# First layer of a two-layer encoder: x transposed on the host, the RMS root applied at eviction or by a spread row, the norm's weight folded into the weight tiles

## The chip, the cores and the metric

The kernel runs on 1 core of one Trainium2 chip. The metric is the device time of one execution in microseconds (us), as the median of several executions. Before the change it is 2655.88 us, the median of 3 executions from 2654.63 to 2658.3 us. One further execution was taken by the hardware profiler; its span, from the first to the last instruction, is 2652.0 us.

## The reference

The model has two layers on x of 2048 rows (frames) by 1024 columns, all in float32. Only the front of the first layer matters for the change:

```python
h = rms_norm(x, a_norm_g)                       # x * rsqrt(mean(x*x, row) + 1e-6) * g
u, v, z = jnp.split(h @ w_in, 3, axis=-1)       # w_in is 1024 x 6144; u, v, z are 2048 wide
u = jax.nn.gelu(u)
v = layer_norm(jax.nn.gelu(v), ln_g, ln_b)
mixed = w_m @ v  (per group of 128 rows, per head of 128 columns)  + b_s
x = x + (u * mixed * jax.nn.silu(z)) @ w_out
```

After that come a shared K/V projection, a chunked band attention layer and a last RMS norm, which the change leaves as they are but for one pair of small tiles.

The RMS norm multiplies each row of x by a scalar, its root, and each column by an element of the weight g. The row scalar can therefore be applied to the rows of a product instead of to the rows of its left operand, and the column weight to the rows of w_in.

## The kernel before, in words

**Products.** Every fp32 product is made of three matmuls on two-part operands: a high part rounded to TensorE's fp32r form and a low part that is the remainder (`mm3`, L110 to L114, whose three matmuls are L111, L112 and L113). `split` (L433) makes the parts: ScalarE (ACT) copies the source into the high part (L434), VectorE (DVE) subtracts it from the source into the low part (L437).

**Stage order.** The first layer's input product is done by a Strassen-Winograd scheme on 2x2 blocks: the rows are paired as even and odd blocks of 128 (16 blocks, so 8 pairs `j`), the 1024 input columns as two halves of 512, and w_in is cut in six slices `n` of 1024 columns: n = 0, 1 are v, n = 2 to 5 hold u and z. For each n there are seven products, the phases `ph`, in the order 1, 2, 6, 5, 7, 4, 3, and for each phase eight steps `j`. A step is 12 matmuls of 128x512: 4 blocks of 128 input columns times 3. For phases 1 and 2 a step of n = 0 makes the product of n = 1 too (24 matmuls). Then the slice "o" makes the layer's output product with steps of 24 matmuls. `run_steps` (L659) writes the order out: at step s it runs the events of s, then the matmuls and the eviction of s, then prepares the left operand of step s + 3 (LOOK = 3), then the weight work due at s. A scheduler at compile time turns this into one instruction queue for each engine; SyncE (SP) issues all DMAs from one queue.

**Left operands S.** With a11, a12 the halves of an even row block and a21, a22 those of the odd one, phase 1 takes a11, phase 2 takes a12, phase 4 takes a22, and phases 6, 5, 7, 3 take sums of blocks. The matmul wants them with the input columns on the partitions, so they are transposed. In n = 0 each of the 7 x 8 = 56 operands is made by `s_split` (L607): four TensorE transposes of 128x128 into PSUM (L611), a split out of PSUM into an S tile (6 buffers), and one step later a store of both parts to HBM (`hsd`, L614, 512 KB). All other steps, and the phases 7, 4 and 5 of n = 0 too, load the stored tile back (`s_load`, L600, DMA at L602).

**The norm.** `block_norm` (L692) does for each of the 16 row blocks: load 128x1024 (L697), ACT squares and sums along the row (L703), DVE adds eps (L709), GpSimd (POOL) raises to -0.5 (L710), DVE multiplies the block by the root and the weight in one instruction (L714). The weight is held as a 128x1024 tile `gab`, loaded once as a broadcast (L699). Only then can the transposes of that block run. Odd blocks go on to `block_c` and `block_d` (L728, L738): POOL makes the three sums of the Winograd scheme (L734 to L736), and the operands of phases 4 and 5 are transposed, split and stored early, during phases 1 and 2.

**Weights T.** `make_t` (L448) loads quarters of w_in (tiles `rw`, 128x1024, 512 KB, L470), combines them on POOL (`comb`, L445) where the phase wants a sum, and splits the result (L434, L437). The result lies in one of 8 buffers, that is two phases of four.

**Eviction.** `evict` (L568) takes a product out of PSUM (4 banks): ACT copies it in phase 1 (L574), DVE adds it to an accumulator in the others (L570). The accumulators are tiles `acc` of 128x512, 25 buffers. PSUM's other 4 banks hold the transposes in n = 0 and n = 1.

## Time and profile before

| | us |
|---|---|
| time of 3 executions | 2654.63, 2655.88, 2658.3 |
| span of the profiled execution | 2652.0 |
| TensorE (PE) busy in it | 2608.0 |
| DVE, ACT, POOL busy in it | 1885.1, 1303.2, 897.2 |
| first product's first matmul starts | 10.82 |

The profile lists each instruction with its engine, its line, and the tiles that it writes and reads ("out<-in"). PE's matmuls are pipelined: their shown durations overlap, so what one costs on PE's line is read from the distance between the starts of neighbours. "Idle before" is the time an engine sat idle before an instruction, with the instruction or DMA whose end released it. Windows give the busy time of each engine in a stretch, with the granted TensorE clock (1 is full speed) and the busy share of the 16 DMA engines.

### The profile page before, as it was taken

To read this page: it belongs to the slowest core of one execution; us is meant where nothing else is said; L and a number is where in the kernel's file an instruction comes from. 1 tells how busy PE (TensorE), PEld (TensorE's weight loads), DVE (VectorE), ACT (ScalarE), POOL (GpSimd) and SP (SyncE) were. 2 spreads that over 40 slices of the span, in tenths; PEclk is the share of its full clock that TensorE was granted. 3 is DMA by queue.
4 is the path that set the end of the run, shared out by engine and by line. 5 is a ranking of instruction groups with operands and counts; after the bars stand their busy time and mean duration, and the time that the engine had idled before them with its cause. 6 is when DMAs were issued, how large, how long until landed. Compare 5 with 4: busy or idle time off the path is not lost. (4 is left out here: it accounts for less than half of the span.)

```text
span 2652.0 us, 37980 instructions
## 1 busy us (share of the span) xinstructions
PE 2608.0 (98%) x12960; PEld 2181.4 (82%) x12960; DVE 1885.1 (71%) x2944; ACT 1303.2 (49%) x2303; POOL 897.2 (34%) x874
## 2 busy tenths in 40 slices
PE   8999999999999999999989999999999999999997
PEld 7888888888888888888878878888888888888886
DVE  5655676865767667757767767777778777877677
ACT  5422243442533434343356456666666655666564
POOL 3611334142152322203234434344332232332245
PEclk9999999999999999999999999999999999999999
DMA  7898998989989869967776597778787666875667
GB/s 286 313 344 329 346 370 323 323 323 338 330 302 313 308 233 324 331 206 270 280 251 214 186 280 229 231 245 263 252 270 254 226 204 224 255 230 161 195 224 251
DMA packets 273856, 718.72 MB, mean 271 GB/s; under 512 B 28800, under 2 KB 68736, under 8 KB 273664
## 3 DMA queue, kind: packets, MB, share of 16 engines
q1 hardware_dynamic: 273664, 716.31, 78.4%
q8 instruction: 103, 1.69, 0.3%
q14 instruction: 89, 0.73, 0.1%
HBM read 531.12 MB, written 174.59 MB: 266 GB/s over the span
## 5 line engine op out<-in xcount | busy, mean ns | idle before, releaser
L111 PE MATMUL P<-T,S 128*128 128x512 f32 x1248 | 496.2, 398 | 2.1 <-ACT S L434 2.1
L112 PE MATMUL P<-T,S 128*128 128x512 f32 x1248 | 488.2, 391 | 1.1 <-DVE T L437 1.1
L113 PE MATMUL P<-T,S 128*128 128x512 f32 x1248 | 488.6, 391 | 0.0
L1417 POOL TENSOR_SCALAR pr<-pr,sl 128x640 f32<-128x640 f32 (+4 forms) x256 | 209.7, 819 | 530.4 <-DVE sl L1416 445.2
L111 PE MATMUL pj<-hh_b,wh_b 128*128 128x512 f32 x768 | 320.4, 417 | 0.0
L113 PE MATMUL pj<-hh_b,wl_b 128*128 128x512 f32 x768 | 305.0, 397 | 1.2 <-DVE wl_b L229 1.1
L112 PE MATMUL pj<-hl_b,wh_b 128*128 128x512 f32 x768 | 303.4, 395 | 0.1
L1413 ACT ACTIVATE pr<-pr,nm 128x640 f32<-128x640 f32 (+4 forms) x256 | 195.5, 764 | 188.1 <-DVE nm L1406 186.6
L113 PEld LDWEIGHTS P<-T,S 128*128 128x128 f32 x1248 | 234.9, 188 | 50.5
L111 PEld LDWEIGHTS P<-T,S 128*128 128x128 f32 x1248 | 235.5, 189 | 46.9 <-ACT S L434 2.3
L112 PEld LDWEIGHTS P<-T,S 128*128 128x128 f32 x1248 | 235.6, 189 | 46.1 <-DVE T L437 1.3
L1438 DVE TENSOR_TENSOR pt<-tp,pt 128x640 fp32r<-128x640 f32 (+4 forms) x256 | 188.4, 736 | 43.7 <-ACT pt L1437 41.1
L1406 DVE CUSTOM_DVE_ANT_0 pr<-s,bias 128x640 f32<-128x640 f32 (+4 forms) x256 | 187.9, 734 | 35.7 <-PE s L1398 29.8
L1437 ACT CAST pt<-tp 128x640 fp32r<-128x640 f32 (+4 forms) x256 | 159.0, 621 | 54.0 <-PE tp L1433 49.8
L1433 PE MATMUL tp<-ident,pr 128*128 128x128 f32 x1120 | 166.7, 275 | 8.6 <-DVE pt L1438 7.3
L113 PEld LDWEIGHTS pj<-hh_b,wl_b 128*128 128x128 f32 x768 | 144.7, 188 | 36.4 <-DVE wl_b L229 3.8
L1433 PEld LDWEIGHTS tp<-ident,pr 128*128 128x128 f32 x1120 | 130.7, 140 | 43.3 <-issue 13.7
L111 PEld LDWEIGHTS pj<-hh_b,wh_b 128*128 128x128 f32 x768 | 145.8, 190 | 18.1 <-ACT wh_b L228 1.6
L1458 PEld LDWEIGHTS pv<-pt,V 128*128 128x128 f32 x896 | 143.3, 189 | 20.8 <-DVE pt L1438 3.9
L112 PEld LDWEIGHTS pj<-hl_b,wh_b 128*128 128x128 f32 x768 | 145.8, 190 | 17.1 <-DVE hl_b L186 0.6
L1458 PE MATMUL pv<-pt,V 128*128 128x256 f32 (+3 forms) x896 | 154.5, 320 | 2.2 <-ACT pt L1437 1.1
L229 DVE TENSOR_TENSOR wl_b<-raw_b,wh_b 128x1024 fp32r<-128x1024 f32 x96 | 120.4, 1255 | 28.5 <-ACT wh_b L228 27.8
(294 smaller groups left out, 5725.9 us busy)
## 6 DMA issues: line engine op xcount, KB each, us to landing
S<-hsd SPq DMA_DIRECT2D x288, 512.0 KB, 5.3
rw<-in_w_a SPq DMA_DIRECT2D x108, 512.0 KB, 6.3
A<-ytd SPq DMA_DIRECT2D x72, 512.0 KB, 5.7
raw_b<-wk SPq DMA_DIRECT2D x72, 512.0 KB, 4.3
hsd<-S SPq DMA_DIRECT2D x56, 512.0 KB, 4.9
V<-vhd SPq DMA_DIRECT2D x56, 512.0 KB, 5.4
bias<-reld SPq DMA_DIRECT2D x64, 320.0 KB, 4.2
va<-vd SPq DMA_DIRECT2D x32, 512.0 KB, 5.5
```

Source lines behind the costliest of these rows:

```text
L111: first = mm(ps, lh, rh, start=first, stop=False)
L112: mm(ps, lh, rl, start=False, stop=False)
L113: mm(ps, ll, rh, start=False, stop=last)
L229: tv(wl[:], raw[:], wh[:].bitcast(F32), op=sub)
L1406: nc.vector.tensor_tensor_reduce(out=pr[:, c0:].rearrange("p (a b) -> p a b", a=nseg), in0=ps[:, :nseg, :w], in1=bias[:, c0:].rearrange("p ...
L1413: nc.scalar.activation(pr[:, c0:], pr[:, c0:], AF.Exp, scale=-1.0, bias=nm[:], accum_out=sl[:])
L1417: nc.gpsimd.tensor_scalar(pr[:, c0:], pr[:, c0:], sl[:], 1.0, op0=ALU.mult, op1=ALU.mult)
L1433: ins = tpose(tp[:, b, :], pr[:, b * P : (b + 1) * P], ident[:])
L1437: nc.scalar.copy(oh, tp[:, b0:5, :].rearrange("p a b -> p (a b)"))
L1438: nc.vector.tensor_tensor(pt[:, 2560 + o + b0 * P : 2560 + o + 640], tp[:, b0:5, :].rearrange("p a b -> p (a b)"), oh.bitcast(F32), op=ALU ...
L1458: mm(po[:, q0 * P : q1 * P], vtl[t, p][:, i, hs], rhs, start=(i == blocks[0] and j == 0), stop=(i == 7 and j == 1),)
```

## The change

The host hands over x^T as a second input `xt`: for each block of 128 rows a 128x1024 array that has the input columns on the partitions, as the matmul wants them. It is the raw x, without root or weight. The blocks of x are loaded from there. The rows of x are still loaded too, but only for the sums of squares (`row_load`, `row_root`); the 16 roots lie side by side in a tile `rs`.

- **Root at eviction.** Phases 1, 2 and 4 take a raw block. Their eviction multiplies by the root of the row block: ACT with a scale (phase 1), DVE's scalar_tensor_tensor (phases 2 and 4).
- **Root by a spread row.** The sums need scaled blocks. For each block ACT makes a 128x128 tile of copies of the root (`row_rep`), one TensorE transpose turns it so that the root of row c stands in column c of all partitions (`row_spread`, into PSUM), and DVE multiplies each half of the block by it (`x_scale`).
- **Weight in the weights.** `gain` multiplies each loaded quarter of w_in by the weight, which now lies along the partitions (`ga`, 128x8): in halves of 512 columns on ACT, for some tiles on DVE. For n = 0, 1 in phase 1 it is part of the split.
- **Parts not stored.** The operands of phases 1 and 2 are not stored as parts. n = 2 to 5 load the raw 128x512 half (256 KB, `xq_load`) into an `acc` tile and split it again (`s_plain`). In n = 0 the operands of phases 4 and 5 are no longer split early: phase 4 loads a raw half, phase 5 loads a sum stored as one fp32 tile (`s1d`), both are split when due, and their parts are stored for n = 1 to 5.
- **Smaller pieces.** `acc` has 23 buffers instead of 25, `gab` is gone, and in the attention two 128x1 tiles become one of 128x2.

The core of the diff:

```diff
         hsd = {
             (ph, j): dram.tile([P, 2, 512], F32, name=f"hsd{ph}_{j}")
-            for ph in range(1, 8) for j in range(NJ)
+            for ph in range(3, 8) for j in range(NJ)
         }
+        s1d = [dram.tile([P, 512], F32, name=f"s1d{j}") for j in range(NJ)]
...
-            return ca.tile([P, 512], F32, tag="acc", name=name, bufs=25)
+            return ca.tile([P, 512], F32, tag="acc", name=name, bufs=23)
...
+            fused = n in (0, 1) and ph == 1
...
+                def gain(t, r, dve=n in (0, 1) and ph == 2):
+                    for i in range(2) if n != "o" and not fused else ():
+                        t_ = t[:, i * 512 : i * 512 + 512]
+                        k = r * 4 + q * 2 + i
+                        if dve:
+                            nc.vector.tensor_scalar(t_, t_, ga[:, k : k + 1], None, op0=mul)
+                        else:
+                            nc.scalar.mul(t_, t_, ga[:, k : k + 1])
+                    return t
+
                 def raw(r, c):
-                    return rows.pop((r, c, q))
+                    return gain(rows.pop((r, c, q)), r)
...
-                    t1 = comb(chain[n](2 + q), raw(0, 1), raw(0, 0))
-                    v = comb(chain[n](q), raw(1, 1), t1)
+                    b22 = raw(1, 1)
+                    t1 = comb(chain[n](2 + q), rows.pop((0, 1, q)), rows.pop((0, 0, q)))
+                    v = comb(chain[n](q), b22, gain(t1, 0, True))
...
+                if fused:
+                    for i in range(2):
...
+                        nc.scalar.mul(hi, src, g_)
+                        nc.vector.scalar_tensor_tensor(
+                            lo, src, g_, hi.bitcast(F32), op0=mul, op1=sub
+                        )
+                    return
...
-                nc.scalar.copy(xa[n, j][:], ps[:])
+                if n != "o":
+                    nc.scalar.mul(xa[n, j][:], ps[:], rs[:, 2 * j : 2 * j + 1])
...
+                    last["evict"] = nc.vector.scalar_tensor_tensor(
+                        c[:], ps[:], rs[:, 2 * j : 2 * j + 1], xa[n, j][:], op0=mul, op1=add
+                    ).ins.name
...
+        def s_parts(n, ph, j, rows):
+
+            t = s_tile(f"S{n}_{ph}_{j}")
+            split(
+                t[:, 0].rearrange("p k c -> p (k c)"), t[:, 1].rearrange("p k c -> p (k c)"),
+                rows, "S",
+            )
+            return t
+
         def s_split(ph, j, rows):
 
-            pt = ptp[0].tile([P, 4, P], F32, tag="t0", name=f"t0_{ph}_{j}", bufs=4)
-            for k in range(4):
-                tpose(pt[:, k, :], rows[:, k * P : k * P + P], ident[:])
-            t = s_tile(f"S0_{ph}_{j}")
-            split(t[:, 0], t[:, 1], pt[:], "S")
+            t = s_parts(0, ph, j, rows)
...
+        def xq_load(n, ph, j):
+            if n:
+                t = acc_tile(f"xq{n}_{ph}_{j}")
+            else:
+                t = p0.tile([P, D], F32, tag="hb", name=f"xq{n}_{ph}_{j}", bufs=3)
+            t = xq[n, ph, j] = t[:, 0:512]
+            if ph == 5:
+                nc.sync.dma_start(t, s1d[j][:])
+            else:
+                r, c = plain[ph]
+                nc.sync.dma_start(t, xt[2 * j + r, :, c * 512 : c * 512 + 512])
+
+        def s_plain(n, ph, j):
+            return s_views(s_parts(n, ph, j, xq.pop((n, ph, j))))
...
-            def scale():
-                nc.vector.scalar_tensor_tensor(t, t, r[:], gab[:], op0=mul, op1=mul)
...
+        def row_root(blk):
+            t = rows_.pop(blk)
+            r = rs[:, blk : blk + 1]
+            ins = nc.scalar.activation(t[:], t[:], AF.Square, scale=1.0 / 32, accum_out=r)
+            last["square"] = ins.ins.name
+            nc.vector.tensor_scalar(r, r, EPS, None, op0=add)
+            ins = nc.gpsimd.tensor_tensor(r, r, mhalf[:], op=ALU.pow)
+            last["power"] = ins.ins.name
+
+        def row_rep(blk):
+            d = rep[blk] = acc_tile(f"rp{blk}")[:, 0:P]
+            nc.scalar.mul(d, ones[:], rs[:, blk : blk + 1])
+
+        def row_spread(blk):
+            tpose(rbc[:, blk, 0], rep.pop(blk), ident[:])
+
+        def x_scale(blk, half):
+            h = (hb if blk % 2 else ha)[blk // 2]
+            h_ = h[:, half * 512 : half * 512 + 512].rearrange("p (k c) -> p k c", k=4)
+            nc.vector.tensor_tensor(
+                h_, h_, rbc[:, blk].broadcast_to([P, 4, P]), op=mul
+            )
...
+        for j in range(NJ):
+            e = 3 + j * 12 // 7
+            if j:
+                put(j - 4, x_load, 2 * j)
+            for blk, s_ in ((2 * j, j - 3), (2 * j + 1, e - 3)):
+                for i, f_ in enumerate((row_load, row_root, row_rep)):
+                    put(s_ + i, f_, blk)
+                at(s_ + 5 - blk % 2, lambda blk=blk: row_spread(blk))
+            put(j + 3, x_scale, 2 * j, 0)
+            put(j + 22, x_scale, 2 * j, 1)
+            put(e - 1, x_load, 2 * j + 1)
+            for i in range(2):
+                put(e + 1, x_scale, 2 * j + 1, i)
+            at(e + 2, lambda j=j: block_c(j))
+            at(e + 4, lambda j=j: block_d(j))
...
+            if ph in (1, 2):
+                return s_plain(n, ph, j)
             return s_load(ph, j, n)
...
+        for n, ph in start:
+            if (n == 0 and ph in (4, 5)) or (n in range(2, 6) and ph < 3):
+                for j in range(NJ):
+                    at(start[n, ph] + j - LOOK - 2, lambda a=(n, ph, j): xq_load(*a))
...
-        "a_norm_g": c(a["a_norm_g"][0]),
+        "xt": c(a["x"][0].reshape(S // P, P, KD, P).transpose(0, 3, 2, 1).reshape(S // P, P, D)),
+        "a_norm_g": c(a["a_norm_g"][0].reshape(KD, P).T),
```

More of the change, by code (lines that the diff above doesn't have):

```diff
@@ L592, in evict @@
                 c = (xa if ph == 4 else ya)[n, j][:]
-                tt(c, ps[:], c, op=add)
+                if ph == 4 and n != "o":
+                    last["evict"] = nc.vector.scalar_tensor_tensor(
+                        c, ps[:], rs[:, 2 * j + 1 : 2 * j + 2], c, op0=mul, op1=add
+                    ).ins.name
+                else:
+                    tt(c, ps[:], c, op=add)
                 done(n, 1 if ph == 4 else 0, 0 if ph == 4 else 1, j, c)
@@ new lines, in trunk_kernel, with x_load, row_load @@
+        nc.gpsimd.memset(ones[:], 1.0)
+        def x_load(blk):
+            if blk % 2:
+                h = hb[blk // 2] = p0.tile([P, D], F32, tag="hb", name=f"hb{blk // 2}", bufs=3)
+            else:
+                h = ha[blk // 2] = p0.tile([P, D], F32, tag="ha", name=f"ha{blk // 2}", bufs=8)
+            nc.sync.dma_start(h[:], xt[blk])
+        def row_load(blk):
+            t = rows_[blk] = p0.tile([P, D], F32, tag="xr", name=f"xr{blk}", bufs=2)
+            nc.sync.dma_start(t[:], x[blk * P : (blk + 1) * P, :])
@@ L939, in trunk_kernel @@
         at(1, lambda: nc.scalar.mul(bsh[:], bsh[:], 0.5))
-        for j in range(NJ):
-            e = j * 7 // 4
-            norm_at(e - 1, e, block_b, j)
-            at(e + 2, lambda j=j: block_c(j))
-            at(e + 4, lambda j=j: block_d(j))
-            at(start[0, 5] + j, lambda j=j: s_split(7, j, h21[j]))
         at(start[1, 6], lambda: [p0x.close(), ptx.close()])
```

99 lines of the change are left out of this document (42 added, 57 removed).

## The prediction

> **What bounds the kernel now.** I read the page first: its busy times, then PE's row of the 40 slices.
>
> ```profile
> PE 2608.0 (98%) x12960; PEld 2181.4 (82%) x12960; DVE 1885.1 (71%) x2944; ACT 1303.2 (49%) x2303; POOL 897.2 (34%) x874
> PE   8999999999999999999989999999999999999997
> ```
>
> An average of 98% does not say which stage is bound, so I cut the span into windows at the first matmul of each phase. Columns: PE, PEld, DVE, ACT, POOL busy, then clock, DMA share, GB/s.
>
> ```profile
> 0.00:11.00 11.00, 7.28 (x37) 6.84 (x37) 2.64 (x4) 5.34 (x8) 2.09 (x10) 1.00 0.79 294
> 11.00:20.00 9.00, 7.92 (x28) 6.02 (x29) 7.67 (x11) 6.64 (x10) 1.10 (x2) 0.81 1.03 411
> 20.00:72.00 52.00, 47.61 (x234) 39.43 (x233) 30.61 (x38) 28.29 (x52) 24.55 (x23) 0.97 0.72 269
> 72.00:123.00 51.00, 51.00 (x260) 42.81 (x259) 35.19 (x53) 24.56 (x42) 37.46 (x29) 1.00 0.85 306
> 123.00:148.00 25.00, 25.00 (x125) 20.67 (x124) 14.23 (x21) 7.02 (x12) 7.59 (x6) 1.00 1.00 381
> 148.00:173.00 25.00, 25.00 (x125) 20.58 (x124) 12.61 (x19) 6.03 (x11) 2.57 (x2) 1.00 0.91 333
> 173.00:195.00 22.00, 22.00 (x99) 18.22 (x98) 16.99 (x25) 6.41 (x9) 0.00 (x0) 1.00 0.99 335
> 195.00:218.00 23.00, 23.00 (x109) 19.05 (x108) 15.19 (x22) 8.04 (x12) 5.05 (x4) 1.00 0.92 318
> 218.00:242.00 24.00, 24.00 (x117) 19.77 (x116) 16.08 (x25) 10.16 (x16) 5.05 (x4) 1.00 0.91 333
> 242.00:351.00 109.00, 109.00 (x483) 90.25 (x482) 65.80 (x100) 24.50 (x34) 27.09 (x19) 1.00 0.94 349
> 351.00:1037.00 686.00, 686.00 (x3316) 573.92 (x3315) 470.07 (x577) 275.30 (x447) 233.08 (x160) 1.00 0.87 314
> ```
>
> The change lies in this stretch. From 72 us to 1037 us PE never pauses, at full clock; n = 1 (242 to 351) does 40 steps in 109.00 us, 2.72 us a step, 0.227 us a matmul. So whatever PE no longer has to do comes off the end one for one, as long as nothing new makes it wait. Only before 72 us does PE idle.
>
> **Term A, the transposes.** They are three groups of one line:
>
> ```profile
> L611 PE MATMUL t<-ident,ha 128*128 128x128 f32 x128 | 19.2, 273 | 0.4 <-DVE ha L714 0.4
> L611 PE MATMUL t<-ident,hb 128*128 128x128 f32 x64 | 9.5, 283 | 4.4 <-DVE hb L714 4.0 <-DVE ra L709 0.3
> L611 PE MATMUL t<-ident,h 128*128 128x128 f32 x32 | 4.8, 272 | 0.0
> ```
>
> 128 + 64 + 32 = 224, or 56 groups of four. What a group costs stands in PE's timeline:
>
> ```profile
> 20.01 0.39 PE L111 MATMUL P<-T,S 128*128 128x512 f32 x1
> 20.23 0.39 PE L112 MATMUL P<-T,S 128*128 128x512 f32 x1
> 20.46 0.60 PE L611 MATMUL t<-ident,ha 128*128 128x128 f32 x4
> 20.82 0.48 PE L113 MATMUL P<-T,S 128*128 128x512 f32 x1
> 21.13 0.39 PE L111 MATMUL P<-T,S 128*128 128x512 f32 x1
> ```
>
> Without the group the L113 would start at 20.46 and the next L111 at 20.69; it starts at 21.13. A group costs 0.44 us: 0.36 for the four, 0.08 in a longer distance after them. Two groups (at 8.10 and 11.29) ran while PE waited anyway and belong to the start, so A = 54 x 0.44 = 23.8 us saved. The Trainium skill, page "TensorE: Matmul & The Clock Gate", section "Part 4: PE-mode transpose", gives about 275 ns for a transpose in a kernel's context. The shown duration agrees (273 ns); taken as a price, an estimate from that page would be 216 x 0.275 = 59 us saved. The starts decide: neighbours overlap, and four cost 0.44.
>
> **Term B, the spread rows.** 16 lone transposes are added, none like them in the trace. Lower bound a quarter of a group's 0.36, 0.09 us; upper bound that plus the whole longer distance, 0.17. I take 0.17, since each stands alone between matmuls: B = 2.7 us lost.
>
> **Term C, the start.**
>
> ```profile
> 1.26 6.44 PE L879 MATMUL wp<-wz 128*128 128x256 f32 x32 [1.26 <-POOL wz L876]
> 4.33 1.06 ACT L703 ACTIVATE jk<-ha 128x1024 bf16<-128x1024 f32 x1 [2.33 <-DMA ha<-in_x]
> 9.24 1.04 ACT L434 CAST T<-rw 128x1024 fp32r<-128x1024 f32 x1
> 10.82 0.50 PE L111 MATMUL P<-T,S 128*128 128x512 f32 x1 [2.07 <-ACT S L434]
> 13.22 1.05 ACT L434 CAST T_hh<-rw 128x1024 fp32r<-128x1024 f32 x1
> ```
>
> x lands by 4.33, but square, root, scaling and transposes put the first matmul at 10.82. Step 0 (24 matmuls, 5.4 us at full rate) ends at 20.01, because its four weight tiles come late: the first is cast at 9.24, the fourth at 13.22. Now nothing but the copy stands between x and S, and the four weight loads have 2 x 512 KB less ahead of them (the broadcast weight and the second x block): 1.05 MB at the first window's 294 GB/s is 3.6 us. The fourth tile then reaches ACT at 9.6; it needs two scaled copies of 0.72 and a low part of about 0.85 (rows below), and the last six matmuls 1.4: step 0 ends at 13.3, not 20.01, 6.7 us earlier. It cannot end before 7.70 (end of the warm-up matmuls) + 5.4 = 13.1. If instead the fused split's extra ACT time (4 x 0.4) and a half-clock spell delay it, 3 us stay. I take 6.5.
>
> **Term D, the stall in phase 1.**
>
> ```profile
> 51.10 1.09 PE L611 MATMUL t<-ident,hb 128*128 128x128 f32 x4 [4.04 <-DVE hb L714]
> 52.41 0.63 PE L112 MATMUL P<-T,S 128*128 128x512 f32 x1
> 52.84 0.63 PE L113 MATMUL P<-T,S 128*128 128x512 f32 x1
> ```
>
> PE waits 4.4 us in window 20:72 (52.00 - 47.61), 4.04 of it here for a normalized odd block; after it the matmuls are 0.43 apart instead of 0.227, and the window's clock of 0.97 makes that 1.6 us. Together 6.0. That wait is gone, since PE no longer reads scaled rows. The new one, the spread, comes two or three steps (11 to 16 us here) behind the ACT copy that it turns. I take 5.0 saved, bounds 0 and 6.0.
>
> **What must stay hidden.** Rows for the new work:
>
> ```profile
> L1102 ACT ACTIVATE wv<-wv,kg 128x512 f32<-128x512 f32 x16 | 11.4, 723 | 15.2 <-DMA wv<-in_w_vv 15.2
> L434 ACT CAST So<-A 128x512 fp32r<-128x512 f32 x64 | 38.7, 620 | 80.4 <-PE Po L113 64.6 <-DMA A<-ytd 15.7
> L437 DVE TENSOR_TENSOR So<-A,So 128x512 fp32r<-128x512 f32 x64 | 53.5, 845 | 21.4 <-ACT So L434 21.3
> L437 DVE TENSOR_TENSOR S<-t,S 128x512 fp32r<-128x512 f32 x56 | 37.1, 685 | 13.0 <-ACT S L434 13.0
> L714 DVE SCALAR_TENSOR_TENSOR ha<-ha,ra,gab 128x1024 f32<-128x1024 f32 x8 | 11.3, 1411 | 7.0 <-POOL ra L710 5.9 <-DMA gab<-in_a_norm_g 1.1
> L570 DVE TENSOR_TENSOR c<-P,x 128x512 f32<-128x512 f32 x48 | 32.6, 682 | 16.9 <-PE P L113 16.9
> 521.30:546.10 24.80, 24.80 (x123) 20.70 (x121) 11.45 (x13) 12.66 (x21) 10.23 (x6) 1.00 0.88 316
> 839.50:865.20 25.70, 25.70 (x132) 21.19 (x130) 24.83 (x33) 11.53 (x19) 6.64 (x5) 1.00 0.99 336
> 865.20:890.00 24.80, 24.80 (x123) 20.70 (x121) 12.65 (x17) 13.06 (x22) 5.04 (x4) 1.00 0.94 330
> ```
>
> *n = 2 to 5.* Each slice gets 16 splits (ACT 0.62, DVE 0.85) in place of loads, and 28 gains on ACT (0.72) and 4 on DVE. The densest place for ACT is phase 1 (third row from below, n = 3): 12.66 + 8 x 0.62 + 8 x 0.72 = 23.4 of 24.8 us. For DVE it is phase 3 (n = 4): 24.83 + 3 x 0.85 = 27.4 of 25.7, 1.7 over, and the phase after it has room (12.65 + 6.8 of 24.8). Operands are prepared 3 steps ahead, 8.2 us, which covers 1.7. DVE at 24.83 of 25.7 did not stop PE before. The gains lengthen the chain load, POOL sum, split by some 2 to 3 us, but the 8 T buffers hold the next phase's weights too, a phase (21.8 us) ahead. Cost 0; uncovered, the two halves of a split are 1.47 us for each of 64 steps. The bytes fall: 64 loads of 256 KB instead of 512.
>
> *n = 0.* DVE loses 16 scalings (1.41 and the like, 24 us) and gets 32 multiplications by a spread row (PSUM and SBUF in, as an eviction: 0.68, 22 us) and 56 low parts out of SBUF instead of PSUM (+0.16, 9 us). Phase 7 (173 to 195) is densest, since its own splits now fall in it: 16.99 + 8 x 0.85 = 23.8 of 21.8, again within the look-ahead. ACT gets 16 copies of 128x128, the scaled evictions (at most +0.13 each) and gains; its densest window is 20:72, 28.29 of now some 43.5, with about 7 us more. POOL's work is the same. In SP's queue, 16 stores of parts for phases 1 and 2 go and 16 loads of rows come. Cost 0.
>
> **Sum.** -23.8 + 2.7 - 6.5 - 5.0 = -32.6 us on the span of 2652.0: 2619.4. The median of the runs, 2655.88, is 3.9 above that span, so the forecast is 2623.3, say 2623. By the page's price for a transpose it would be about 2588. The terms' bounds alone (B 1.4 to 2.7, C 3 to 6.9, D 0 to 6.0) give 2621 to 2632; the queues of the later stages may come out in another order, and PE's idle time of 44.0 us (2652.0 - 2608.0) lies mostly there, so I allow 8 us either way: 2613 to 2640.
>
> **Rivals.**
>
> *DMA or DVE takes over in n = 0 (2634).* From 123 to 242 us the DMA moves 25 x 381 + 25 x 333 + 22 x 335 + 23 x 318 + 24 x 333 GB/s x us = 40.5 MB. The change takes out 24 loads of parts (12.6 MB), and moves in 16 stores of phases 4 and 5 (8.4) and 16 loads of 256 KB (4.2): the same bytes. PE would need about 109 us, so 373 GB/s, next to the 381 at a share of 1.00. At 335 GB/s it takes 121 us, and about 11 us come back. For it: the shares of 0.91 to 1.00. Against it: PE did not wait at 1.00, stores can lag, loads are issued five steps ahead.
>
> *The spread makes PE wait on DVE (2655, no change).* The 16 spread rows share four PSUM banks, four blocks in each, and a later spread of a bank must come after DVE's multiplication has read the earlier ones: PE in order behind DVE. Today's one such wait cost 4.04 + 1.6 us; six of that size eat the 33. The Trainium skill, page "PSUM — Partial Sum Buffer", section "PSUM bank collisions raise a hardware error", says that two engines may not touch one bank at once, so software must order them. No wait of that kind is in this trace. Against it: a step is 5.4 us there, and DVE has 21 us idle in 52.
>
> *The splits of phases 1 and 2 sit behind ACT's waits (2673, slower).*
>
> ```profile
> ACT T L434 <- DMA rw<-in_w_a: 24.4, 6, 10.3
> ```
>
> ACT already waits for weight loads, up to 10.3 us, and was harmless because S came by DMA. Now each gain on ACT can wait so, with S splits and scaled evictions queued behind it, for which PE waits. A wait of 10.3 exceeds the 8.2 of look-ahead by 2.1; six in each of the four slices cost 50 us. It turns the sign from four in each slice. Against it: the mean wait today is 4.1, and few.
>
> That the change does not do what it says is no rival: the transposes are out of the program.
>
> **How the numbers follow.** Forecast 0.62; DMA or DVE in n = 0 0.20; spread 0.07 (of this 0.02 with a smaller gain left); ACT's waits 0.09; the page's price 0.02. Faster by over 0.2% (5.3 us, about what a measurement of this kernel can tell from no change): 0.62 + 0.20 + 0.02 + 0.02 = 0.86; same 0.05; slower 0.09. The range 2613 to 2642 takes in the forecast and the first rival and leaves 0.18 out.
>
> **What would show it.** Right: no transposes but 16 in n = 0; the first product's matmul near 8 us and step 0 done near 13 to 14; phases 6 to 3 of n = 0 at 21.8 us each; n = 2 to 5 still without PE idle, at the same 172 us a slice; from 1037 us on (then about 1004) all as before. Wrong: PE idle behind the spread or its DVE reads; PE idle behind S in phases 1 and 2 of n = 2 to 5; matmuls 0.43 apart anywhere after 20 us.

## The result and the profile after

The kernel after takes 2672.43 us (median of 4 runs, 2671.83 to 2675.79) against 2655.35 us of the kernel before on the same chip: ratio 1.0063, 95% interval 1.0049 to 1.0077. It is slower by 17 us; the forecast was 2623. The profiled execution has a span of 2670.1 us against 2652.0. One of the nine executions of the version s3 below ran at a granted clock of 0.556 and took 4288.6 us; its ratio leaves that one out, and its profile is that of s5, the same kernel once more.

TensorE (PE) lost the work that it was meant to lose and is nevertheless done later. From the page of after, the busy row:

```profile
PE 2595.7 (97%) x12752; PEld 2161.6 (81%) x12752; DVE 1972.7 (74%) x3060; ACT 1438.0 (54%) x2539; POOL 907.5 (34%) x875
```

PE's busy time fell by 12.3 us (2608.0 before), while DVE gained 87.6 and ACT 134.8. Windows of after, cut at the first matmul of each stretch (PE, PEld, DVE, ACT, POOL busy, then clock, DMA share, GB/s): n = 0, n = 1, n = 2 to 5, and below them n = 0 and n = 2 to 5 of before.

```profile
8.40:220.40 212.00, 201.73 (x881) 162.51 (x882) 166.18 (x246) 124.25 (x209) 92.28 (x72) 1.00 0.88 321
220.40:333.20 112.80, 109.69 (x482) 89.92 (x481) 65.99 (x101) 38.80 (x57) 23.60 (x19) 1.00 0.94 346
333.20:1055.60 722.40, 697.88 (x3318) 578.30 (x3316) 546.16 (x657) 371.80 (x617) 241.45 (x160) 0.99 0.79 275
```

```profile
10.80:242.10 231.30, 225.82 (x1084) 186.83 (x1085) 148.88 (x208) 97.35 (x160) 83.37 (x70) 0.99 0.88 319
350.90:1037.10 686.20, 686.20 (x3316) 574.08 (x3315) 470.27 (x577) 275.49 (x447) 233.08 (x160) 1.00 0.87 314
```

Put together, with the same cuts in the trace of before:

| stretch | before, us | after, us | difference | forecast |
|---|---|---|---|---|
| up to the first matmul | 10.8 | 8.4 | -2.4 | in n = 0 |
| n = 0 | 231.3 | 212.0 | -19.3 | -32.6 with the row above |
| n = 1 | 108.8 | 112.8 | +4.0 | 0 |
| n = 2 to 5 | 686.2 | 722.4 | +36.2 | 0 |
| from "o" on | 1614.9 | 1614.5 | -0.4 | 0 |

The sum is +18.1, the difference of the spans. The first slice gained two thirds of what was forecast; the four slices that repeat it lost more than that. In these, PE did not wait at all before. What it waits for now (waits of PE in 333.2 to 1055.6 us of after; columns: waited for, us in total, times, longest):

```profile
PE P L114 <- DVE c L607: 6.6, 5, 2.4
PE mx L115 <- DVE vl L441: 5.0, 2, 4.2
PE ty L912 <- DVE y L932: 4.7, 2, 2.3
PE mx L114 <- ACT m L901: 3.4, 1, 3.4
PE P L114 <- DVE x L596: 1.8, 1, 1.8
PE ty L912 <- ACT th L930: 1.7, 2, 1.0
PE P L116 <- DVE S L441: 0.4, 1, 0.4
PE P L114 <- DVE x L628: 0.4, 2, 0.2
PE ty L912 <- ACT yo L914: 0.3, 1, 0.3
```

The row of `S` is the one to remember: for the new splits themselves PE waits 0.4 us in all. It waits 8.8 us for evictions that should have emptied a PSUM bank (`c`, `x`), 8.4 us for the mixing stage's operands and results (`vl`, `m`), and 6.7 us for what it is to transpose (`y`, `th`, `yo`). All of them share DVE's and ACT's queues with the splits. The idle time is 24.5 us (722.40 - 697.88); the other 11.7 us of the loss are longer matmuls. Four spells, 17.1 us together, ran at half clock during or right after such waits; PE is busy in 15.5 us of them, so by an estimate from these figures they cost some 7.7 us. Where the other 4 us lie is not shown.

By the starts of the phases' first matmuls, the loss of n = 3 to 5 lies in phases 1 and 2, the phases with the splits (25.5 of 28.3 us). In n = 2 these two phases together lose nothing, and 7.3 of its 8.0 us come in phases 6 and 5, right behind them.

### The profile page after: what moved, and what is told of

Read it like the earlier page. It is cut to its first block, busy times and chain, and to the rows that moved or that the text cites. A ratio compares the mean times of both kernels' runs of the same rounds, so it can differ in the third digit from the quotient of the medians.

```text
span 2670.1 us, 37974 instructions
## 1 busy us (share of the span) xinstructions
PE 2595.7 (97%) x12752; PEld 2161.6 (81%) x12752; DVE 1972.7 (74%) x3060; ACT 1438.0 (54%) x2539; POOL 907.5 (34%) x875
## 5 line engine op out<-in xcount | busy, mean ns | idle before, releaser
L1489 POOL TENSOR_SCALAR pr<-pr,ns 128x640 f32<-128x640 f32 (+4 forms) x256 | 207.7, 812 | 528.5 <-DVE ns L1488 437.5
L1485 ACT ACTIVATE pr<-pr,ns 128x640 f32<-128x640 f32 (+4 forms) x256 | 195.5, 764 | 188.8 <-DVE ns L1478 187.9
L114 PEld LDWEIGHTS pj<-hh_b,wh_b 128*128 128x128 f32 x768 | 145.3, 189 | 18.1 <-ACT wh_b L231 1.8
L489 ACT ACTIVATE rw<-rw,ga 128x512 f32<-128x512 f32 x152 | 103.0, 718 | 93.8 <-DMA rw<-in_w_a 88.3
```

The source lines that it names most:

```text
L114: first = mm(ps, lh, rh, start=first, stop=False)
L489: nc.scalar.mul(t_, t_, ga[:, k : k + 1])
L1485: nc.scalar.activation(pr[:, c0:], pr[:, c0:], AF.Exp, scale=-1.0, bias=nm, accum_out=sl)
L1489: nc.gpsimd.tensor_scalar(pr[:, c0:], pr[:, c0:], sl, 1.0, op0=ALU.mult, op1=ALU.mult)
```

## The experiments

Theory D says that the 64 repeated splits and the gains fill DVE; theory W, the forecast's third rival, that ACT's waits for weights delay the splits; the forecast for n = 0 itself (transposes come off one for one) is tested too. Later expectations add theory A (ACT's half of a split is late), theory C (the split is a link too many: at first the chain of two engines, later a split of any kind between load and PE) and theory L (the raw loads and their order in the queue). The edits are shortened: `...` marks what is left out. All ratios are against runs of the kernel before on the same chip (2655.1 to 2656.1 us).

### The first slice

**Only the transposes removed from the kernel before.**

```
-            for k in range(4):
-                tpose(pt[:, k, :], rows[:, k * P : k * P + P], ident[:])
...
-            split(t[:, 0], t[:, 1], pt[:], "S")
+            split(t[:, 0]..., t[:, 1]..., rows, "S")
```

> The kernel before without its 224 transposes: the split reads the block as it lies (the block is then not transposed, so the products are of other numbers; this run is for its time). Term A says 24 us come off, as 0.44 us for each group of four: 2655 - 24 = 2631. If instead VectorE's low parts out of SBUF (they came out of PSUM) are stretched by GpSimd and hold TensorE up already here, less than 15 us come off: 2640 or more.

2662.02 us, 1.0021 (1.0012 to 1.0031): not faster. The first slice takes 232.3 us instead of 231.3:

```profile
10.60:242.90 232.30, 208.62 (x865) 168.36 (x865) 162.61 (x205) 96.77 (x158) 93.92 (x70) 0.94 0.85 313
```

PE is busy 17 us less and waits 18 us more (23.7 idle), mostly for loaded S tiles (8.3 us), for ACT's evictions (7.9) and for DVE's (5.8). So PE's transposes were not the only thing that set this slice's length. The time lies in the range of the second expectation (2640 or more), but DVE, its reason, ended the smaller part of these waits.

**Only the 16 stores of phases 1 and 2 removed from the kernel before** (slices 2 to 5 load other stored parts).

```
+            if ph > 2:
                 later(1, lambda: paced(nc.sync.dma_start(hsd[ph, j][:], ...)))
```

> The kernel before with all its transposes and its whole norm; only the 16 stores of the parts of phases 1 and 2 (8.4 MB in the first slice) are left out, and slices 2 to 5 load the stored parts of phases 6 and 7 in their place (so these products take other left operands). If the first slice's stores set its time and not the transposes: its 231.3 us become 212 to 220 and the whole 2636 to 2645. If transposes and stores bind alike: 2648 to 2656.

2665.03 us, 1.0031 (1.002 to 1.0041), above both expectations; n = 0 takes 240.2 us. Fewer bytes did not help while PE had the transposes: it was busy 229.34 of the 240.20 us, and the order of the queues came out worse at one transposing step (waits for DVE's split `S` of 8.3 us in all).

**The kernel after, but with the parts of phases 1 and 2 stored by n = 0 and loaded by n = 2 to 5**; a second kernel leaves out the gains of n = 2 to 5 as well, a third leaves out only these gains.

```
-                return s_views(s_parts(0, 1, j, a11))
+                return s_split(1, j, a11)
...
-            if ph in (1, 2):
-                return s_plain(n, ph, j)
...  (second and third kernel)
-                    for i in range(2) if n != "o" and not fused else ():
+                    for i in range(2) if n in (0, 1) and not fused else ():
```

> The changed kernel, but phases 1 and 2 are stored as parts by n = 0 and loaded by n = 2 to 5, as before. The changed kernel takes 2672; its slices n = 1 to 5 lose 40 us against before. Theory D (VectorE is overfull: 64 more low parts out of SBUF, each 0.68 us alone and 1.8 beside GpSimd): most of the loss in n = 2 to 5 goes, 2640 or less. Theory W (ScalarE waits for weight loads in its 152 gains, and what stands behind it is late): the loss stays but for a few us, 2662 to 2672.

> Both edits of the last two runs: parts stored and loaded, and no weight in n = 2 to 5. If the splits and the gains together make the loss of the later slices, whatever their shares, it is gone: 2672 - 36 to 40 = 2632 to 2636; what is left against the forecast of 2623 is then n = 0. If it stays over 2645, something else is lost there (23 accumulators instead of 25, or the order of the queues).

> The changed kernel, but the norm's weight is left out of n = 2 to 5 (u and z are computed without it): no gain instructions there, the splits of phases 1 and 2 stay. Theory W (ScalarE's waits for weight loads): most of the 40 us goes, 2640 or less. Theory D (VectorE overfull by the splits): only the 16 gains on VectorE go, 2662 to 2672.

Parts stored: 2665.63 us, 1.0041 (1.0027 to 1.0055). Stored and no gains: 2660.02, 1.0012 (1.0002 to 1.0021). Only no gains: 2664.48, 1.0039 (1.0024 to 1.0054). Windows of the one with stored parts, n = 0 and n = 2 to 5:

```profile
7.90:241.20 233.30, 212.04 (x880) 168.03 (x880) 167.20 (x248) 126.43 (x210) 89.25 (x72) 0.95 0.88 324
356.60:1049.50 692.90, 688.48 (x3318) 574.65 (x3316) 482.39 (x594) 341.83 (x556) 236.51 (x160) 1.00 0.87 311
```

and n = 2 to 5 of the one without gains too:

```profile
356.10:1041.70 685.60, 685.60 (x3316) 573.76 (x3315) 475.31 (x578) 279.22 (x448) 236.78 (x160) 1.00 0.88 316
```

The time of the first lies where theory W put it and that of the third where theory D put it. The second, at 2660 instead of the 2632 to 2636 expected, shows why whole times don't decide here: the stores take away the gain of n = 0. Two things follow from the windows. With stored parts n = 2 to 5 take 692.9 us instead of 722.4, and without gains 685.6, as before: the repeated splits cost 29.5 us, the gains 7.3. Taken in the other order, the gains are worth 3.6 us (718.8 us without them) and the splits 33.2. And n = 0 with the transposes gone but the stores kept takes 233.3 us instead of 212.0. With the transposes PE alone is busy for 226 to 229 us of this slice, and with the stores it takes 232 to 233 us even without them; its 19 us came only when both were gone. Whether the stores hold it by their bytes or by their places in SP's queue is not shown.

**No spread, no scaling of the sums** (the sums then lack the root).

```
-                at(s_ + 5 - blk % 2, lambda blk=blk: row_spread(blk))
...
-            put(j + 3, x_scale, 2 * j, 0)
```

> The changed kernel without the spread of the root and the 32 multiplications by it (the sums of blocks are then of raw blocks). In n = 0, phase 2 takes 53.1 us for 43.5 us of matmuls, and PE waits 5.0 us behind the spread and its multiplications and 4.6 behind VectorE's evictions. If the spread is the rival of the prediction (TensorE behind VectorE), n = 0 ends 8 to 10 us earlier, 2663. If VectorE is overfull there anyway, only 2 to 4 us: 2669.

2678.42 us, 1.0088 (1.0073 to 1.0103): slower than after, against both expectations. Phase 2 of n = 0 takes 62.2 us instead of 53.1. PE waits for DVE's eviction, and DVE stood at the place in its queue where it multiplies a weight sum by the gain, until GpSimd (POOL) had made that sum. PE's timeline, then DVE's waits from 78 to 97 us:

```profile
81.49 0.80 PE L114 MATMUL P<-T_hl,S 128*128 128x512 f32 x1 [9.00 <-DVE c L607]
```

```profile
DVE ch L487 <- POOL ch L449: 16.6, 2, 10.8
```

POOL was busy for 52.0 us of this phase's 62.2 (39.7 of 53.1 in after). The price of the spread itself is therefore not measured, but a first case of the pattern is: an eviction late because something else stands at the head of its engine's queue.

### The slices that repeat

**The parts stored once, by n = 2, which splits them anyway; n = 3 to 5 load them.**

```
-            if ph in (1, 2):
+            if n == 2 and ph in (1, 2):
                 return s_plain(n, ph, j)
...
+            later(1, lambda: paced(nc.sync.dma_start(hsd[ph, j][:], ...)))
```

> The changed kernel, but n = 2 stores the parts of phases 1 and 2 that it splits, and n = 3 to 5 load them. The run with stored parts showed what n = 3 to 5 cost with loads: 173.3, 177.2 and 171.8 us instead of 181.2, 182.2 and 180.7; n = 0 should stay at the 212 us of the changed kernel, since it stores nothing more. If the splits cost in each slice by themselves, 2672 - 22 = 2650, faster than before. If the loss only moves to where the 16 stores are (n = 2), 2660 or more.

2656.01 us, 1.0003 (0.9994 to 1.0012), between the two expectations: the loss against the kernel before is gone, and the first slice stays short (211.7 us). n = 2 takes 182.8 us (170.4 before), n = 3 to 5 take 524.4 (515.8 before).

**DVE's half of the split given to ACT; the same given to POOL.** In the first the low part is a copy, so it isn't the remainder.

```
-            nc.vector.tensor_tensor(lo, src, hi.bitcast(F32), op=sub)
+            nc.scalar.copy(lo, src)
```

> The changed kernel, but in phases 1 and 2 of n = 2 to 5 ScalarE writes the low part too, as a second copy (so the low part is wrong); VectorE does nothing for these 64 splits, ScalarE 0.62 us more for each. Theory D (VectorE overfull): the loss of the splits (30 us by the run with stored parts) goes, 2642 to 2650. Theory W (the wait for the raw half, or ScalarE): no better than the changed kernel, 2665 to 2680.

> The changed kernel, but GpSimd makes the low part in phases 1 and 2 of n = 2 to 5, which is the same arithmetic. GpSimd is busy 241 of the 722 us of n = 2 to 5 and gets 64 subtractions of about 1.5 us. Theory D: VectorE has its 60 us back, but its own instructions with two operands from SBUF run beside GpSimd more often (1.8 us instead of 0.68): 2648 to 2662. Theory W: as the changed kernel, 2670.

ACT: 2665.23 us, 1.004 (1.0025 to 1.0055). POOL: 2708.03 us, 1.0194 (1.0177 to 1.0211). The first gives back 7 us of 17, less than theory D asked, and lies where theory W put it; the second is slower than either expectation, a warning about POOL, whose subtraction takes 1710 ns in the mean where DVE's takes 625 to 1791.

**One half of the split left out altogether.**

```
no low part:   in_order("S", nc.scalar.copy(hi, src));  product takes hi twice
no high part:  nc.vector.tensor_tensor(lo, src, src, op=sub);  product takes lo twice
```

> The kernel after, but the 64 repeated splits of slices 2 to 5 in phases 1 and 2 make the high part alone (ScalarE's copy); the product takes the high part twice, so the output leaves the low part of x^T out there. Loads, ScalarE's work and the 3 matmuls stay as they are; VectorE loses 64 subtractions (64 x 0.92 = 59 us of its time) and, with them, every place at which VectorE's queue stands until ScalarE's copy is done. Theory D (VectorE has no room for them): 2640 to 2648. Theory C (the chain of the two engines, each standing at the other's place in its queue): about 2645 as well. Theory A (it is ScalarE's half that is late): 2662 to 2675. Theory L (the raw loads and their order in the queue): 2662 to 2675.

> The mirror of it: VectorE's subtraction stays, of the raw tile from itself, and waits for the load alone; ScalarE's 64 copies (64 x 0.72 = 46 us of its time) are gone; the product takes the one part twice, so x^T is left out of these products. Theory D: 2660 to 2672. Theory A: 2640 to 2648. Theory C: about 2645, since VectorE no longer stands behind ScalarE's copy though it does all its work; low here and low in the run without the low part together are C. Theory L: 2662 to 2675.

Without DVE's half 2673.25 us, 1.0064 (1.0046 to 1.0082); without ACT's half 2674.07, 1.0079 (1.006 to 1.0098). Both as slow as with the two halves. D and A fall, each as a matter of that engine's share alone, and so does C as a chain of two engines, which asked for about 2645 in both; L asked for these times and is tested next. Phase 2 of n = 5 in the two kernels, the one without the low part first:

```profile
905.50:938.40 32.90, 27.10 (x121) 21.84 (x120) 16.53 (x19) 21.51 (x38) 15.11 (x10) 0.95 0.51 184
```

```profile
900.60:935.70 35.10, 28.47 (x121) 23.33 (x122) 28.70 (x28) 18.43 (x33) 16.81 (x10) 0.90 0.53 186
```

The phase took 24.7 us before. In the first kernel DVE is busy for half of it and the phase is long all the same.

**Raw loads without splits, and splits without raw loads.** The first keeps the 64 loads into `acc` tiles and takes stored parts of other phases as S; the second splits the identity, which lies in SBUF.

```
loads only:   return s_load(ph + 5, j, n)
splits only:  split(t[:, 0], t[:, 1], ident[:] (4 times), "S")
```

> The kernel after; in slices 2 to 5 the 64 raw 256 KB loads into acc tiles stay at their places, read only by a one-column operation of VectorE, but the splits go: S is loaded as two stored parts of 512 KB, those of phases 6 and 7 (so phases 1 and 2 of these slices take other left operands than they should). Theory L (raw loads and the 64 acc tiles that they occupy): stays at 2660 to 2675. Theory C (a split of any kind between the load and TensorE): 2635 to 2648.

> The mirror of it: the 64 splits stay, both halves at full size, but their source is the identity that lies in SBUF from the start (read four times over, so these products leave x^T out); the raw loads and their acc tiles are gone. Theory L: 2635 to 2648. Theory C: 2660 to 2675, since ScalarE and VectorE have the same work and TensorE waits for both. In between: each pays a part.

Loads only: 2663.92 us, 1.0032 (1.0019 to 1.0044), above the 2635 to 2648 of theory C (a split of any kind) and within the 2660 to 2675 of theory L. The trace says where: its waits lie in phase 1 of n = 4 and n = 5 and right behind it, 12.4 of 18.0 us for S loads, with the extra loads in the same queue, and 5.3 us behind the one-column operation, which stands in DVE's queue until its load is there. n = 2 and 3 take 343.7 us together (342.3 before). The stretch with the wait in n = 4:

```profile
678.50:714.20 35.70, 26.68 (x135) 22.01 (x133) 15.93 (x22) 19.73 (x33) 12.91 (x8) 0.98 0.83 300
```

Splits only: 2679.25 us, 1.009 (1.0072 to 1.0108), above the range of theory C and far from that of L, and n = 2 to 5 take 733.2 us. So the splits carry the loss without any load; the loads in this form, with more bytes than after has, cost in two places of their own.

**The splits one step earlier.**

```
-    if ph in (1, 2): return s_plain(n, ph, j)          # 3 steps ahead
+    ts[start[n, ph] + j - LOOK - 1]: s_early(n, ph, j) # 4 steps ahead
```

> The kernel after; in phases 1 and 2 of slices 2 to 5 the raw halves are loaded and split one step earlier, 4 steps ahead of their product instead of 3 (10.9 us instead of 8.2; of the 6 S tiles 5 are then in use). Nothing else changes. If the splits only come late by less than a step, behind the short waits of VectorE and ScalarE (the stalls of TensorE are 0.7 to 4.2 us each): most of the 36 us come back, 2640 to 2655. If the two engines run short for longer than a step, or their queues come out worse whatever the lead: 2664 to 2675.

2676.19 us, 1.0075 (1.0058 to 1.0092): nothing comes back. It could not: PE waits only 0.4 us for the splits in after. More lead puts them further ahead of the evictions in the queues.

**What is late, measured in each trace.** An eviction can start when its product is done, and the next step's first matmul starts then too. The distance from that matmul to the eviction's start is the eviction's lag. Over the 32 evictions of phase 2 in n = 2 to 5, worked out from the instruction lists:

| kernel | mean lag, us | longest | n = 2 to 5, us |
|---|---|---|---|
| before | 0.8 | 3.8 | 686.2 |
| stored, no gains | 1.0 | 3.7 | 685.6 |
| stored | 1.3 | 5.4 | 692.9 |
| loads without splits | 2.0 | 7.0 | 710.4 |
| after, low part by ACT | 4.8 | 9.4 | 716.1 |
| after, no gains | 6.6 | 13.2 | 718.8 |
| after | 6.8 | 12.5 | 722.4 |
| no low part | 6.8 | 14.8 | 727.3 |
| one step earlier | 7.2 | 12.7 | 724.7 |
| no high part | 7.4 | 13.2 | 725.7 |
| splits without loads | 8.2 | 12.8 | 733.2 |
| after, low part by POOL | 8.5 | 16.2 | 755.1 |

The products have 4 PSUM banks and a step is 2.7 to 3.1 us, so an eviction may lag about three steps, some 8 to 9 us, before PE has no bank to go on with (an estimate from these figures). Before, that reserve was hardly touched. In every kernel that splits in these slices it is used up at the densest places. How it is used up can be read in DVE's timeline of after, phase 2 of n = 3 (start, us, line, operation, and in brackets the idle time before it with its releaser):

```profile
545.64 0.75 DVE L877 SCALAR_TENSOR_TENSOR va<-va,lmv,lg 128x512 f32<-128x512 f32 x1 [3.24 <-DMA va<-vd]
546.31 1.22 DVE L441 TENSOR_TENSOR T<-ch,T 128x1024 fp32r<-128x1024 f32 x1
547.45 0.74 DVE L878 SCALAR_TENSOR_TENSOR va<-va,lrs,lb 128x512 f32<-128x512 f32 x1
548.11 1.78 DVE L441 TENSOR_TENSOR S<-xq,S 128x512 fp32r<-128x512 f32 x1
549.82 0.74 DVE L607 SCALAR_TENSOR_TENSOR c<-P,rs,x 128x512 f32<-128x512 f32 x1
550.48 1.63 DVE L441 TENSOR_TENSOR T<-ch,T 128x1024 fp32r<-128x1024 f32 x1
552.03 0.74 DVE L877 SCALAR_TENSOR_TENSOR va<-va,lmv,lg 128x512 f32<-128x512 f32 x1
552.80 1.67 DVE L878 SCALAR_TENSOR_TENSOR va<-va,lrs,lb 128x512 f32<-128x512 f32 x1
554.39 1.75 DVE L441 TENSOR_TENSOR S<-xq,S 128x512 fp32r<-128x512 f32 x1
556.06 0.74 DVE L607 SCALAR_TENSOR_TENSOR c<-P,rs,x 128x512 f32<-128x512 f32 x1
556.73 1.21 DVE L441 TENSOR_TENSOR vl<-va,vh 128x1024 fp32r<-128x1024 f32 x1
```

DVE stands 3.24 us at a load for the mixing stage, and from there on it has no gap; between two evictions (`c`) lie a split of T, two operations on `va` and a split of S, 6.2 us, where PE takes 3.1. The same place before, with DVE waiting for PE:

```profile
558.68 0.69 DVE L570 TENSOR_TENSOR c<-P,x 128x512 f32<-128x512 f32 x1 [1.99 <-PE P L113]
```

and what PE, in after, makes of it:

```profile
557.99 0.58 PE L115 MATMUL mx<-vl,ws 128*128 128x256 f32 x1 [4.16 <-DVE vl L441]
...
559.23 0.63 PE L114 MATMUL P<-T,S 128*128 128x512 f32 x1
559.65 0.63 PE L115 MATMUL P<-T,S 128*128 128x512 f32 x1
```

PE waits 4.16 us for `vl`, and the matmuls that follow are 0.42 apart instead of 0.23. In the kernel without the low part DVE has no split to do, and the place is lost another way: it stands for a load, and the eviction stands behind it.

```profile
914.05 0.75 DVE L882 SCALAR_TENSOR_TENSOR va<-va,lmv,lg 128x512 f32<-128x512 f32 x1 [12.58 <-DMA va<-vd]
...
918.22 0.74 DVE L607 SCALAR_TENSOR_TENSOR c<-P,rs,x 128x512 f32<-128x512 f32 x1
```

That load was issued late, because SP's queue stood before it from 901 to 907 us at a weight load. There it waited for POOL's sum `rw`, and POOL for ACT's gain:

```profile
900.79 0.43 SPq L676 DMA_DIRECT2D xq<-in_xt  x1
906.63 0.33 SPq L475 DMA_DIRECT2D rw<-in_w_a  x1
907.01 0.42 SPq L676 DMA_DIRECT2D xq<-in_xt  x1
907.53 0.38 SPq L873 DMA_DIRECT2D va<-vd  x1
```

Waits of DVE for these loads (`va<-vd`) set the two groups of kernels apart. In n = 2 to 5 they come to 20.4 us before, 21.0 and 21.3 with stored parts; in the eight kernels of the table that split, to 33.5 to 68.6 us (38.9 in after), and with loads and no splits to 0.9. Whether they begin the trouble or follow from it is not shown.

The Trainium skill, page "TensorE: Matmul & The Clock Gate", section "Architectural detail: the array is 16× 32×32, not 1× 128×128", has the queues of ScalarE and VectorE as strictly first in, first out. Both of DVE's timelines agree with it: an eviction whose product had been done for 11.7 us (at 556.06) and one of 9.3 us (at 918.22) did not pass their neighbours.

**Gains of the version with parts from slice 2 moved.** The weight's factor inside the split for phases 1, 2 and 3 of n = 2 to 5 (s3, and s5 for its profile); all of ACT's gains given to POOL (s4); s3 with the splits of n = 2 one step earlier (e2).

```
s3:  fused = n != "o" and (ph in (1, 2, 3) if n > 1 else ph == 1)
s4:  nc.gpsimd.tensor_scalar(t_, t_, ga[:, k : k + 1], 1.0, op0=mul, op1=mul)
```

> Parts stored from slice 2 on, as in the version that gave 2656.0, and the norm's weight of phases 1, 2 and 3 of slices 2 to 5 not multiplied in place by ScalarE ahead of the split but inside it: ScalarE's high part takes the factor and VectorE's subtraction takes it too. ScalarE loses 48 gains of 0.72 = 34 us of work and the wait for the weights' load that stands at their place in the queue; VectorE's split becomes the operation with a per-row scalar, at the same length or longer. If the 8.6 us that slices 3 to 5 are still over the kernel before come from ScalarE's gains: 2648 to 2652. If from VectorE's share: 2656 or more.

> Parts stored from slice 2 on, and every gain that ScalarE made given to GpSimd. ScalarE is freed as in the run beside it, but GpSimd gets 152 more operations, and VectorE's subtractions beside a busy GpSimd took 1.8 us instead of 0.68 in the trace of after. If ScalarE's queue is the cause: 2648 to 2652. If VectorE's share is: 2660 to 2675.

> The version with parts stored from slice 2 on and the weight's factor inside the split, for its profile: 2645 to 2651; slices 3 to 5 at 172 us each, as in the kernel before, and what is left over it in slice 2 (some 10 us).

> The same one step of lead for slice 2 of the version that stores the parts from slice 2 on and has the weight's factor inside the split (2648 and 2650 so far). That slice is 10 us over the kernel before. If its splits are late by less than a step: 2638 to 2645. If the S tiles, held by their stores, are what is short: 2648 to 2656.

s3: 2648.13 us, 0.9973 (0.9962 to 0.9983), faster than both kernels; s5: 2649.95. s4: 2663.82, 1.0042 (1.0023 to 1.0061). e2: 2650.75, 0.9979 (0.997 to 0.9988), also faster than both kernels and no better than s3; that its S tiles are what is short, as the second expectation has it, is not shown by that. n = 2 and n = 3 to 5 of s5:

```profile
333.80:514.60 180.80, 173.78 (x821) 143.50 (x820) 137.46 (x176) 85.95 (x145) 63.28 (x42) 0.99 0.90 327
514.60:1032.20 517.60, 516.05 (x2499) 431.10 (x2498) 363.37 (x455) 240.27 (x401) 174.21 (x118) 1.00 0.87 310
```

n = 3 to 5 are 1.8 us over their length before (515.8); n = 2, the only slice that still splits, pays 10.4 us, and n = 1 has 5 us of its own. So of the 22.0 us by which n = 1 starts earlier in s5, 4.9 are left when "o" starts (1032.2 us against 1037.1).

## Why the prediction was wrong, point by point

**What bounds the kernel.** "Whatever PE no longer has to do comes off the end one for one, as long as nothing new makes it wait" was right as a rule, and its condition failed.

**Terms A and B** were sized well as work: PE's busy time in n = 0 fell from 225.82 to 201.73 us, 24.1 us, against 23.8 - 2.7 = 21.1; two half-clock spells of 3.4 us that are gone explain up to 3.4 of it. As time they were not independent of the stores, since without the transposes alone the slice kept its length. That the change took the stores out as well is why they came through; the forecast put the stores at nothing, so this was luck.

**Term C** (6.5 saved) was too high. The first matmul is at 8.41 us, as forecast near 8; step 0 ends at about 14.6, and step 1, for which 20.01 was the start before, begins at 15.74 after a wait for ACT's half of its split. 4.3 us were saved there:

```profile
8.41 0.50 PE L114 MATMUL P<-T,S 128*128 128x512 f32 x1 [0.34 <-ACT T L520]
...
14.38 0.39 PE L116 MATMUL P<-T_hh,S 128*128 128x512 f32 x1
15.74 0.50 PE L114 MATMUL P<-T,S 128*128 128x512 f32 x1 [0.96 <-ACT S L438]
```

**Term D** (5.0 saved) failed. The old wait is gone, but n = 0 has more idle time than before, 10.3 us (212.00 - 201.73) instead of 5.5. 4.5 us of it, in four waits, are the second rival, the spread behind DVE and ACT; two of the four:

```profile
69.05 0.30 PE L785 MATMUL rbc<-ident,rp 128*128 128x128 f32 x1 [2.11 <-DVE ha L790]
95.81 0.33 PE L785 MATMUL rbc<-ident,rp 128*128 128x128 f32 x1 [0.91 <-ACT rp L782]
```

The rival needed six waits of 5.6 us. "Two or three steps (11 to 16 us here) behind the ACT copy that it turns" was not enough cover. Another 4.5 us are waits for DVE's evictions (`c` 2.5, `x` 2.1), which the forecast had not in n = 0.

**What must stay hidden, n = 2 to 5: "Cost 0".** This is the step that failed, and it carries the sign: +36.2 us. It summed each engine's busy time over a phase, found it below the phase's length or 1.7 us over it, and covered the rest by the 8.2 us with which operands are prepared ahead. That cover held for the splits, for which PE waits 0.4 us. It was never there for what shares their queue: evictions, which have no lead, only the PSUM banks' reserve, and the mixing stage. The forecast's own alternative, "uncovered, the two halves of a split are 1.47 us for each of 64 steps", priced the wrong instruction. The busy times were too low as well. The split out of SBUF was put at 0.85 and took 0.93 on DVE in the mean, some 0.68 and some 1.78, and other operations stretched too. In phase 2 of n = 3 the forecast's way of counting gives DVE 17.20 + 8 x 0.85 = 24.0 us; it was busy for 29.23 of 33.70. The mean of the splits in after, and this phase before and after:

```profile
L441 DVE TENSOR_TENSOR S<-xq,S 128x512 fp32r<-128x512 f32 x80 | 73.7, 931 | 4.9 <-ACT S L438 4.9
546.10:570.80 24.70, 24.70 (x121) 20.88 (x120) 17.20 (x24) 11.69 (x20) 6.18 (x5) 1.00 0.94 326
536.30:570.00 33.70, 28.20 (x121) 22.59 (x120) 29.23 (x28) 20.50 (x37) 19.81 (x14) 0.90 0.81 274
```

**n = 0: "Cost 0"** held in phases 5, 7, 4 and 3, at 21.8 us each as forecast. The first rival (DMA takes over there, 121 us for phases 6 to 3) did not happen: they took 111.8. **n = 1** was to stay and lost 4.0 us, 3.1 of them waits for loaded S tiles at a DMA share of 0.94, as high as before.

**The third rival** (2673, ACT's waits) came out at the measured time and in the right place, but for the wrong reason in part. ACT's waits for weights are there (n = 2 to 5: 54.9 us in 25 waits, the longest 14.5). But without any gain the loss in these slices falls by 3.6 us only, and its condition, PE waiting for S or for ACT's evictions, is not met: 0.4 us for S, none for ACT's evictions. That its total fits is luck: it put 50 us on these slices against 32.6 saved elsewhere, and the runs show 36.2 against 18.1. It had 0.09.

**What stays open.** That splits in these slices make evictions late is shown; which queue begins it at each place is not. Two ways were seen: a stretch of DVE without gaps behind a wait for a load (after, and without the high part), and loads issued late behind POOL and ACT (without the low part). The order that the scheduler gave the queues changed a little with the splits: in n = 3 the first eviction of phase 2 stands behind 50 of the 128 operations on `va` instead of 46, in n = 4 behind 83 instead of 78, in n = 5 behind 115 instead of 114; with stored parts the counts are those of before. So the work of the splits and this new order were never tested apart. A kernel with the evictions' places fixed by hand, and one that gives the raw halves a pool of their own, were not tried; so how much of the 36 us a better order would save is not known. Nor is it shown why the gain as part of the split costs less than the gain in place.

## What to carry to other kernels

When an operand that came by DMA is made by an engine instead, don't ask only whether it comes in time; look at what else is in that engine's in-order queue, and at the instructions with the least lead, here the evictions and the mixing stage's operands. Measure the evictions' lag before and compare it with what the PSUM banks allow: a stage where DVE is busy for half the time (16.53 of 32.90 us without the low part) may still have no room for a queue that stands. And before counting a saving on the busiest engine, look for a second limit of nearly the same length; here the transposes came off only together with the stores.

## What the runs showed of the hardware

DVE's operations with two tensors in SBUF have no fixed length. In after the subtraction for S takes 0.68 us and the operations on `va` 0.74 when they run freely, and up to 1.8 us otherwise; the eviction `c`, which reads PSUM, keeps 0.74 (48 of them, mean 739 ns). Of the 248 subtractions for S and operations on `va`, 75 took over 0.76 us. In 74 of these a 128x512 operation of POOL was already running when they started, and they ended 0.55 us after its end. Five others met one with over 0.2 us left and stayed short. Each came in a row of DVE operations that had begun before POOL's, and there POOL's operation was the long one (3.29 us at 375.47, where others of its kind take 1.28 at the shortest). The Trainium skill, page "SBUF — State Buffer", section "SBUF: two separate sides", states that such a DVE operation and a GpSimd operation that reads SBUF exclude one another for a whole instruction. The trace agrees, in both directions.

The clock drops after quite short waits, and where a wait falls matters. A wait of 1.78 us at 405.03 was followed, 1.3 us later, by 3.4 us of matmuls 0.43 apart:

```profile
406.35 0.63 PE L116 MATMUL P<-T,S 128*128 128x512 f32 x1
406.77 0.63 PE L114 MATMUL P<-T,S 128*128 128x512 f32 x1
```

The half-clock spells of after from there on start at 406.23, 556.42, 703.19, 750.98, 1399.51, 1426.82 and 1611.14 us (a last one stands at the program's end), that is 44, 87, 101, 291, 299 and 353 times 3.413 us after the first. Each of the first four followed a stretch of this grid in which PE had idled for 1.8 to 2.6 us. Waits of 3.35 us (to 435.00), 2.33 (to 884.62) and 2.44 (to 929.17) lie across a boundary of the grid, with 1.7 to 1.9 us in one stretch, and were followed by no spell. Since 1.78 us brought a spell and 1.9 us did not, the idle time in one stretch alone does not settle it.
